# Residual additions of a decoder layer done by accumulating DMAs from GpSimd instead of loads and VectorE additions

## The chip, the core and the metric

The kernel runs on one core of a Trainium2 chip. The core has a matrix engine (TensorE, PE in the profile), three engines for elementwise work (VectorE DVE, ScalarE ACT, GpSimd POOL), and a queue engine, SyncE (SP), that here only starts transfers. Each engine runs its own list of instructions strictly in order and waits on semaphores for others. Transfers are carried by 16 DMA engines; what an engine's list holds is only the start of a transfer. Data lies in SBUF as 128 partitions by so many elements. The metric is the device time of one execution in microseconds.

## The reference

One decoder layer in float32: 1024 tokens, width 1024, one batch. A token mixer with three branches (pooling, a linear-attention recurrence, cross-attention into 256 memory tokens) is merged by gates and projected by `w_o`; then a gated feed-forward part with a short convolution follows. Both parts end in a norm and a residual addition; these two additions are what the change touches:

```python
merged = gates[:, :, 0] * y_pool + gates[:, :, 1] * y_rwkv + gates[:, :, 2] * y_mem
x = x + rms_norm(merged @ w_o[l], norm_mix_post[l])
h = rms_norm(x, norm_ffn_pre[l])
u = causal_dwconv(h @ w_ffn_up[l], conv_w[l], conv_b[l])
u_gate, u_val = jnp.split(u, 2, axis=-1)
f = (jax.nn.gelu(u_gate, approximate=True) * u_val) @ w_ffn_down[l]
x = x + rms_norm(f, norm_ffn_post[l])
```

## The kernel before

Activations are kept transposed, channels on the partitions: a tensor of 1024 channels and 512 tokens is eight blocks of 128 x 512. The tokens go in two halves, n = 0 and n = 1. Every product is made of three TensorE passes: weights and activations are split into a high part in a matmul type (`whi`, `h2h`, `mgh`) and the rest (`wlo`, `h2l`, `mgl`). A weight tile of 128 x 256 comes in by a load on SP (`wraw`, line 152), ScalarE casts it to `whi` (line 126), GpSimd subtracts to make `wlo` (line 129), and TensorE multiplies (lines 163 to 165). Two sets of such tiles alternate, three deep for `wraw` and four deep for `whi` and `wlo`.

Around the first residual the order in the program is: `merge(0)` and `wo_gemm(0)` make the eight blocks `o` of the first half; then `merge(1)` for the second half runs block by block (gate products on VectorE at lines 879 and 880, their split into `mgh` on ScalarE and `mgl` on VectorE, lines 119 and 120), and the generator `wo_residual(0)` is driven between its blocks. It takes the norm's factor `rs` (ones-matmul at line 1025, ScalarE at line 195), and for each of eight blocks k: scales `o[k]` (VectorE, line 1061), adds the block of the input x (line 1063) loaded into one of two buffers `xt` (SP, line 1060), stores the sum to DRAM as `d_x1` (SP, line 1064), and takes its square (ScalarE, lines 1016 and 1019) into a running sum `s2` (VectorE, line 1020). This is place A, 1337 to 1362 us.

`wo_residual(1)` does the same for the second half, beside the first tiles of the up projection (weights `in_w_fup`); there x comes as one load of 2 MB into `xts` (line 1054). This is place B, 1419 to 1450 us. `wo_norm` then scales `o` and splits it into `h2h` and `h2l`.

The tail, place C, 2110 to 2154 us: `down_pass` has left the first half's sums in `accs[0]`. While the last blocks of the second half run on TensorE (`half_down`), VectorE scales the eight blocks of `accs[0]` (line 1306), adds the stored `d_x1` (line 1307), which a load of 2 MB brought in long before (line 1292), and SP stores them to the output (line 1308).

The program text is not the order of the lists: the Tile layer schedules each engine's instructions by dependences, by priority in the text and by its own estimate of when each is ready. Buffers are rotated by tags, and a waiting instruction holds everything behind it on its engine.

Of the kernel before, what the change touches and what calls it, by code (L numbers as in the profile page):

```python
# [8 lines left out]
F32 = mybir.dt.float32  # L9
FR = mybir.dt.float32r  # L10
AF = mybir.ActivationFunctionType
ALU = mybir.AluOpType
# [4 lines left out]
P = 128  # L17
T = 1024
D = 1024
KC = D // P  # L20
# [22 lines left out]
def trunk_kernel(ctx: ExitStack, tc: tile.TileContext, xT, memT, pvec, w_in, w_kv, w_upd, w_upg,  # L43
                 w_pool, w_ppool, w_pmem, w_prwkv, w_o, w_fup, w_fdn, out):
    nc = tc.nc
    V, A, G, PE, SP = nc.vector, nc.scalar, nc.gpsimd, nc.tensor, nc.sync
# [9 lines left out]
    def dtile(shape, name):  # L56
        return dram.tile(shape, F32, name=name, tag=name)
# [7 lines left out]
    d_x1 = dtile([8, P, T], "d_x1")  # L65
# [6 lines left out]
    def col(name, i):  # L72
        o, w = PV[name]
        return pv[:, o + i:o + i + 1]
# [18 lines left out]
    for lo in (0, 64):  # L93
        s = slice(lo, lo + 64)
# [3 lines left out]
    for lo in (0, 64):  # L98
        s = slice(lo, lo + 64)
# [119 lines left out]
    for k in range(KC):  # L219
        tag = ("X01", "X11", "HV", "HV")[k // 2]  # L220
        if k in (0, 2, 4):
            xt = rw.tile([P, 4 if k == 4 else 2, T], F32, name=f"xr{k}", tag=tag)
# [560 lines left out]
    for hd in range(4):  # L783
        for t0, _ in HALVES:
            s = slice(t0, t0 + 512)
# [49 lines left out]
    for j in range(8):  # L835
        ws = load_w(w_pmem[j], 4)
        for n, (t0, _) in enumerate(HALVES):
            s = slice(t0, t0 + 512)
# [4 lines left out]
    for j in range(8):  # L843
# [4 lines left out]
        for n, (t0, _) in enumerate(HALVES):  # L848
            s = slice(t0, t0 + 512)
# [161 lines left out]
    ow = ow_ctx.enter_context(tc.tile_pool(name="ow", bufs=1))  # L1011
    h2h, h2l = [], []

    def sumsq(acc, src, first, eng):
        if first:
            A.activation(acc, src, AF.Square)
        else:
            sq = wp.tile([P, 512], F32, name="sq", tag="st", bufs=3)[:, :src.shape[-1]]
            A.activation(sq, src, AF.Square)
            eng.tensor_tensor(acc, acc, sq, op=ALU.add)  # L1020

    def norm(pool, acc, after=None):
        w = acc.shape[-1]
        ps = pss.tile([P, 512], F32, name="psn", tag="s")[:, :w]
        mm = PE.matmul(ps, ones, acc, start=True, stop=True)
        if after is not None:
            tc.add_manual_dep(mm.ins, after.name, nosync, reason="order")
        rs = pool.tile([P, 512], F32, name="rs", tag="rs", bufs=1)[:, :w]
        rstd(rs, ps, 0)
        return rs  # L1030
# [15 lines left out]
    def wo_residual(n, after=None):  # L1046

        s = slice(n * 512, n * 512 + 512)
        o = os_[n]
        rs = norm(ow, sss[n], after)  # L1050
        s2 = ow.tile([P, 512], F32, name="s2", tag="ss", bufs=2)
        if n:
            xts = hf.tile([P, KC, 512], F32, name="xts", tag="h2h1")
            SP.dma_start(xts, xT[:, s].rearrange("(k p) t -> p k t", p=P))
        for k in range(KC):
            if n:
                xt = xts[:, k]
            else:
                xt = ow.tile([P, 512], F32, name="xt", tag="xt", bufs=2)
                SP.dma_start(xt, xT[k * P:(k + 1) * P, s])  # L1060
            V.scalar_tensor_tensor(o[k], o[k], col("g_mix_post", k), rs, op0=ALU.mult,
                                   op1=ALU.mult)
            V.tensor_tensor(o[k], o[k], xt, op=ALU.add)
            SP.dma_start(d_x1[k][:, s], o[k])
            sumsq(s2, o[k], k == 0, V)
            if k % 2:
                yield s2
# [25 lines left out]
    merge(1, range(1, 3))  # L1093
    table(LN_EXP)
    res = wo_residual(0, pin)
    s2 = next(res)
    table(SIGMOID)
# [4 lines left out]
    hf = ctx.enter_context(tc.tile_pool(name="hf", bufs=1, side="right"))  # L1102
# [7 lines left out]

    pairs = [[first(0)]]
    res = wo_residual(1, last_mm[0])
    s2 = next(res)
    pairs[0].append(first(NF))
# [136 lines left out]
    def half_down(n, h, j, last):  # L1251

        qs = slice(256 * h, 256 * h + 256)
        ps = psg.tile([P, 2, 256], F32, name="psg", tag=f"g{j // 2 % 2}")
        for e in range(2):
            gemm(weights(j + e), hidden(n, qs), ps=ps[:, e])
        a_ = accs[n][:, j:j + 2, qs]
        V.tensor_tensor(a_, a_, ps, op=ALU.add)
        sq = wp.tile([P, 2, 256], F32, name="sq", tag="st", bufs=3)
        ss = ss3[1 - h].rearrange("p (e t) -> p e t", e=2)  # L1260
        if j == 0:
            A.activation(ss, a_, AF.Square)
        else:
            A.activation(sq, a_, AF.Square)
            if not last:
                V.tensor_tensor(ss, ss, sq, op=ALU.add)
        for e in range(2):
            A.activation(a_[:, e], a_[:, e], AF.Identity, scale=col("g_ffn_post", j + e))
        return ss, sq
# [20 lines left out]
    def load_x1(n):  # L1290
        t = hf.tile([P, KC, 512], F32, name="xt", tag=("h2h1", "h2l1")[n])
        SP.dma_start(t, d_x1[:, :, n * 512:n * 512 + 512].rearrange("k p t -> p k t"))
        return t

    down_pass(0)
    down_pass(4)
    xts = [load_x1(n) for n in range(2)]

    rs0 = None
    for j in range(0, 8, 2):  # L1300
        parts = half_down(1, 0, j, False)
        if j == 0:
            rs0 = norm(fa, ss3[0], last_mm[0])
        for k in range(j, j + 2):
            a_ = accs[0][:, k]
            V.scalar_tensor_tensor(a_, a_, col("g_ffn_post", k), rs0, op0=ALU.mult, op1=ALU.mult)
            V.tensor_tensor(a_, a_, xts[0][:, k], op=ALU.add)
            SP.dma_start(out[k * P:(k + 1) * P, 0:512], a_)
    for j in range(0, 8, 2):
        last = half_down(1, 1, j, j == 6)  # L1310
# [52 lines left out]
def build(arrays):  # L1363
    import numpy as np
    import concourse.bacc as bacc

    nc = bacc.Bacc("TRN2", target_bir_lowering=False, num_devices=1)
    aps = {n: nc.dram_tensor(f"in_{n}", a.shape, mybir.dt.from_np(a.dtype), kind="ExternalInput").ap()
           for n, a in arrays.items()}
    out = nc.dram_tensor("out_T", (D, T), F32, kind="ExternalOutput").ap()  # L1370
    with tile.TileContext(nc) as tc:
        trunk_kernel(tc, **aps, out=out)
    return nc
# [10 lines left out]
```

## Time and profile before

| what | us |
|---|---|
| median of 3 runs (2151.31 to 2157.1) | 2152.29 |
| the profiled execution | 2155.78 |
| its span | 2153.8 |
| TensorE busy | 2081.9 (97%) |
| VectorE busy | 1259.8 (58%) |
| ScalarE busy | 1048.6 (49%) |
| GpSimd busy | 825.0 (38%) |

The span is the time from the first to the last record of the execution; its own time is 2.0 us longer. The granted clock of TensorE was 0.989 of full speed on the mean. "Busy" counts the instructions that compute: the start of a transfer is not busy time on the engine that starts it. TensorE's matmuls are pipelined, so their lengths overlap; the distance of two starts tells the pace, 0.23 us for a matmul of 512 columns at full clock. A row of the timeline that ends in brackets tells how long the engine had been idle before, and which engine and line ended that.

### The profile page before, as it was taken

How to read it: one execution, taken by the hardware profiler on the slowest of the kernel's cores; microseconds unless marked ns; L12 is line 12 of the kernel's file. 1: busy time of each engine (PE TensorE's matmuls, PEld its weight loads, DVE VectorE, ACT ScalarE, POOL GpSimd, SP SyncE). 2: the span in 40 equal slices, each digit the busy share in tenths (PEclk: the TensorE clock that was granted, in tenths of full speed). 3: DMA queues.
4: the chain of work that ended last, by engine and by line, in shares of the span. 5: the costliest groups of instructions: out<-in, count | busy, mean ns of one | idle time of the engine just before them, and what ended most of it. 6: DMA issues, size and time to landing. Idle time of an engine off the chain costs nothing. (4 is left out here: it accounts for less than half of the span.)

```text
span 2153.8 us, 34571 instructions
## 1 busy us (share of the span) xinstructions
PE 2081.9 (97%) x12426; PEld 1594.7 (74%) x12426; DVE 1259.8 (58%) x2031; ACT 1048.6 (49%) x2241; POOL 825.0 (38%) x969
## 2 busy tenths in 40 slices
PE   7999999999999999999999999999999999989998
PEld 4777766776677676866777788777688777768887
DVE  6277437653656356734695434769677777732426
ACT  4584347623862376334565344446444444443423
POOL 6422112111212111201122355556688888843210
PEclk9999999999999999999999999999999999999999
DMA  4312111120212021214345343643322222275532
GB/s 145 131 39 80 61 63 58 63 72 30 89 55 87 21 84 59 89 42 165 127 138 173 123 131 119 189 135 113 105 74 86 76 74 88 75 236 157 162 103 79
DMA packets 170795, 215.04 MB, mean 100 GB/s; under 512 B 17408, under 2 KB 124544, under 8 KB 170624
## 3 DMA queue, kind: packets, MB, share of 16 engines
q1 hardware_dynamic: 170624, 212.84, 30.3%
q8 instruction: 98, 1.61, 0.3%
q14 instruction: 73, 0.60, 0.1%
HBM read 163.48 MB, written 49.28 MB: 99 GB/s over the span
## 5 line engine op out<-in xcount | busy, mean ns | idle before, releaser
L129 POOL TENSOR_TENSOR wlo<-wraw,whi 128x256 fp32r<-128x256 f32 x552 | 476.4, 870 | 1113.7 <-ACT whi L126 965.3
L126 ACT CAST whi<-wraw 128x256 fp32r<-128x256 f32 x560 | 219.6, 404 | 361.4 <-PE psg L164 159.1
L165 PE MATMUL psg<-hh,wlo 128*128 128x512 f32 x928 | 381.8, 411 | 7.3 <-POOL wlo L129 7.1
L163 PE MATMUL psg<-hh,whi 128*128 128x512 f32 x928 | 380.5, 410 | 0.0
L164 PE MATMUL psg<-hl,whi 128*128 128x512 f32 x928 | 378.3, 408 | 0.7 <-DVE hl L120 0.7
L165 PEld LDWEIGHTS psg<-hh,wlo 128*128 128x128 f32 x928 | 175.3, 189 | 54.7 <-POOL wlo L129 14.1
L163 PEld LDWEIGHTS psg<-hh,whi 128*128 128x128 f32 x928 | 175.3, 189 | 41.2 <-ACT tBN L195 0.8
L164 PEld LDWEIGHTS psg<-hl,whi 128*128 128x128 f32 x928 | 175.3, 189 | 40.9 <-DVE hl L120 1.3
L959 POOL TENSOR_TENSOR wt<-a,wt 128x256 fp32r<-128x256 f32 x136 | 133.8, 1012 | 28.7 <-ACT wt L958 28.7
L120 DVE TENSOR_TENSOR fl<-fraw,fh 128x512 fp32r<-128x512 f32 x82 | 61.3, 768 | 134.7 <-ACT fh L119 134.5
L163 PE MATMUL psd<-fh,whi 128*128 128x512 f32 x288 | 114.8, 399 | 9.0 <-DVE z L1004 9.0
L164 PE MATMUL psd<-fl,whi 128*128 128x512 f32 x288 | 114.7, 398 | 1.4 <-POOL fl L120 1.4
L165 PE MATMUL psd<-fh,wlo 128*128 128x512 f32 x288 | 114.5, 398 | 0.0
L959 POOL TENSOR_TENSOR wt<-sm,wt 128x256 fp32r<-128x256 f32 x102 | 106.7, 1065 | 14.5 <-ACT wt L958 14.2
L165 PE MATMUL psf<-h2h,wt 128*128 128x512 f32 x272 | 108.4, 398 | 1.3 <-POOL wt L959 1.2
L163 PE MATMUL psf<-h2h,wt 128*128 128x512 f32 x272 | 106.9, 393 | 1.2 <-ACT wt L958 1.2
L164 PE MATMUL psf<-h2l,wt 128*128 128x512 f32 x272 | 106.8, 393 | 0.0
L977 DVE SCALAR_TENSOR_TENSOR d<-z,pv,d 128x1023 f32<-128x1023 f32 x68 | 91.3, 1342 | 23.8 <-ACT d L975 11.4
L958 ACT CAST wt<-sm 128x256 fp32r<-128x256 f32 x102 | 37.9, 404 | 117.6 <-POOL sm L944 112.6
L165 PE MATMUL psf<-t,wt 128*128 128x512 f32 x204 | 81.2, 398 | 2.1 <-POOL wt L959 1.8
L164 PE MATMUL psf<-t,wt 128*128 128x512 f32 x204 | 80.3, 394 | 0.0
L163 PE MATMUL psf<-t,wt 128*128 128x512 f32 x204 | 80.2, 393 | 0.0
(403 smaller groups left out, 4596.0 us busy)
## 6 DMA issues: line engine op xcount, KB each, us to landing
wraw<-in_w_in SPq DMA_DIRECT2D x240, 128.0 KB, 2.3
fraw<-d_f SPq DMA_DIRECT2D x84, 256.0 KB, 3.1
a<-in_w_fup SPq DMA_DIRECT2D x128, 128.0 KB, 2.4
d_zg<-st SPq DMA_DIRECT2D x48, 256.0 KB, 2.7
wraw<-in_w_fdn SPq DMA_DIRECT2D x88, 128.0 KB, 2.4
wraw<-in_w_fup SPq DMA_DIRECT2D x80, 128.0 KB, 2.4
d_f<-d SPq DMA_DIRECT2D x17, 512.0 KB, 3.3
wraw<-in_w_prwkv SPq DMA_DIRECT2D x64, 128.0 KB, 2.3
```

Source lines behind the costliest of these rows:

```text
L120: return (lo_eng or V).tensor_tensor(lo, src, hi.bitcast(F32), op=ALU.subtract)
L126: A.copy(hi, src)
L129: (V if lo_on_dve[0] else G).tensor_tensor(lo, src, hi.bitcast(F32), op=ALU.subtract)
L163: first = PE.matmul(ps, wh, xh, start=start, stop=False)
L164: PE.matmul(ps, wh, xl, start=False, stop=False)
L165: last_mm[0] = PE.matmul(ps, wl, xh, start=False, stop=stop).ins
L958: A.copy(w[0][:, us], src[u])
L959: G.tensor_tensor(w[1][:, us], src[u], w[0][:, us].bitcast(F32), op=ALU.subtract)
L977: V.scalar_tensor_tensor(d[:, n:], z[:, :T - n], col(cw, j), d[:, n:], op0=ALU.mult, op1=ALU.add)
```

## The change

In `wo_residual` and in the tail, the loads of x (or of `d_x1`) into SBUF and the VectorE additions go. Instead GpSimd starts, for each block, a transfer of 128 x 512 from DRAM that adds what it reads to the block in SBUF (`accum_op=ALU.add`). That is 24 loads and additions in all, in 10 load instructions, replaced by 24 transfers. The stores and squares that followed the additions now follow the transfers' landing. In `xts` of the tail only the second half's load is left.

```diff
@@ -1049,18 +1049,10 @@
         o = os_[n]
         rs = norm(ow, sss[n], after)
         s2 = ow.tile([P, 512], F32, name="s2", tag="ss", bufs=2)
-        if n:
-            xts = hf.tile([P, KC, 512], F32, name="xts", tag="h2h1")
-            SP.dma_start(xts, xT[:, s].rearrange("(k p) t -> p k t", p=P))
         for k in range(KC):
-            if n:
-                xt = xts[:, k]
-            else:
-                xt = ow.tile([P, 512], F32, name="xt", tag="xt", bufs=2)
-                SP.dma_start(xt, xT[k * P:(k + 1) * P, s])
             V.scalar_tensor_tensor(o[k], o[k], col("g_mix_post", k), rs, op0=ALU.mult,
                                    op1=ALU.mult)
-            V.tensor_tensor(o[k], o[k], xt, op=ALU.add)
+            G.dma_start(o[k], xT[k * P:(k + 1) * P, s], accum_op=ALU.add)
             SP.dma_start(d_x1[k][:, s], o[k])
             sumsq(s2, o[k], k == 0, V)
             if k % 2:
@@ -1294,7 +1286,7 @@
 
     down_pass(0)
     down_pass(4)
-    xts = [load_x1(n) for n in range(2)]
+    xts = [None, load_x1(1)]
 
     rs0 = None
     for j in range(0, 8, 2):
@@ -1304,7 +1296,7 @@
         for k in range(j, j + 2):
             a_ = accs[0][:, k]
             V.scalar_tensor_tensor(a_, a_, col("g_ffn_post", k), rs0, op0=ALU.mult, op1=ALU.mult)
-            V.tensor_tensor(a_, a_, xts[0][:, k], op=ALU.add)
+            G.dma_start(a_, d_x1[k][:, 0:512], accum_op=ALU.add)
             SP.dma_start(out[k * P:(k + 1) * P, 0:512], a_)
```

The change also moves instructions in the lists. GpSimd's list at A and B, the two lists compared (a minus stands for before, a plus for the change; line 1055 of the changed kernel is the new transfer, `wlo` are the weight splits):

```order
-L129 TENSOR_TENSOR wlo<-wraw,whi 128x256 x206
...
+L129 TENSOR_TENSOR wlo<-wraw,whi 128x256 x108
+L1055 DMA o<-in_xT 128x512 x6
+L129 TENSOR_TENSOR wlo<-wraw,whi 128x256 x3
+L1055 DMA o<-in_xT 128x512
+L129 TENSOR_TENSOR wlo<-wraw,whi 128x256
+L1055 DMA o<-in_xT 128x512
+L129 TENSOR_TENSOR wlo<-wraw,whi 128x256 x53
+L1055 DMA o<-in_xT 128x512 x6
+L129 TENSOR_TENSOR wlo<-wraw,whi 128x256 x2
+L1055 DMA o<-in_xT 128x512
+L129 TENSOR_TENSOR wlo<-wraw,whi 128x256
+L1055 DMA o<-in_xT 128x512
```

What was one run of 206 splits is now cut by two groups of eight transfers, of which six each stand without a split between them.

At A, the same list of the changed kernel by buffer numbers (`wlo_13275` to `wlo_13293` are the four tiles of one weight block in the order in which TensorE reads them, `wlo_13344` to `wlo_13356` belong to the next block):

```order
L129 TENSOR_TENSOR wlo_13275<-wraw_13273,whi_13274 128x256
L129 TENSOR_TENSOR wlo_13281<-wraw_13279,whi_13280 128x256
L129 TENSOR_TENSOR wlo_13287<-wraw_13285,whi_13286 128x256
L1055 DMA o_12522<-in_xT 128x512
L129 TENSOR_TENSOR wlo_13344<-wraw_13342,whi_13343 128x256
L1055 DMA o_12522<-in_xT 128x512
L129 TENSOR_TENSOR wlo_13350<-wraw_13348,whi_13349 128x256
L129 TENSOR_TENSOR wlo_13356<-wraw_13354,whi_13355 128x256
L129 TENSOR_TENSOR wlo_13293<-wraw_13291,whi_13292 128x256
```

The block's last tile, `wlo_13293`, now stands behind all eight transfers and behind three tiles of the next block.

At B, SP's list before (`d_x1` are the stores of the residual, `wraw` the weight loads of the up projection, `a21` a load for later):

```order
L1064 DMA d_x1_81<-o_13480 128x512 x2
L152 DMA wraw_14274<-in_w_fup 128x256
L935 DMA a21_15221<-in_w_fup 128x512
L152 DMA wraw_14280<-in_w_fup 128x256
L1064 DMA d_x1_81<-o_13481 128x512
L152 DMA wraw_14231<-in_w_fup 128x256
L1064 DMA d_x1_81<-o_13481 128x512
L152 DMA wraw_14364<-in_w_fup 128x256
```

And the same place of the changed kernel (line 1056 is the store; the weight `wraw_14213` here is `wraw_14231` above, since the buffer numbers differ by 18 there):

```order
L1056 DMA d_x1_81<-o_13464 128x512
L935 DMA a21_15203<-in_w_fup 128x512
L1056 DMA d_x1_81<-o_13464 128x512
L1056 DMA d_x1_81<-o_13465 128x512 x2
L1056 DMA d_x1_81<-o_13466 128x512 x2
L1056 DMA d_x1_81<-o_13467 128x512 x2
L152 DMA wraw_14213<-in_w_fup 128x256
L152 DMA wraw_14250<-in_w_fup 128x256
```

The stores now stand together, and the load of `wraw_14213` and the loads after it stand behind all eight; before, loads stood between the stores.

## Rows read from the trace of the kernel before

**Rows 1.** The page: engines' busy time, data queue, weight cast, up-projection loads.

```profile
PE 2081.9 (97%) x12426; PEld 1594.7 (74%) x12426; DVE 1259.8 (58%) x2031; ACT 1048.6 (49%) x2241; POOL 825.0 (38%) x969
...
q1 hardware_dynamic: 170624, 212.84, 30.3%
...
L126 ACT CAST whi<-wraw 128x256 fp32r<-128x256 f32 x560 | 219.6, 404 | 361.4 <-PE psg L164 159.1
...
wraw<-in_w_fup SPq DMA_DIRECT2D x80, 128.0 KB, 2.4
```

**Rows 2.** Stretches: length, busy us (and instructions) of each engine, granted clock, DMA.

```profile
1337.00:1362.00 25.00, 25.00 (x109) 20.07 (x108) 23.93 (x32) 16.41 (x34) 14.90 (x14) 1.00 0.67 214
1362.00:1380.00 18.00, 15.72 (x59) 11.77 (x58) 7.98 (x10) 6.11 (x16) 11.37 (x14) 0.91 0.87 276
1419.00:1450.00 31.00, 30.43 (x128) 23.66 (x127) 25.28 (x36) 15.08 (x33) 17.73 (x20) 1.00 0.48 158
2110.00:2141.00 31.00, 30.89 (x225) 28.91 (x223) 22.94 (x37) 15.10 (x30) 0.00 (x0) 1.00 0.19 73
```

**Rows 3.** Timeline of TensorE, 1367 to 1375: start, length, operation, [idle before, releaser].

```profile
1367.55 0.39 PE L165 MATMUL psg<-mgh,wlo 128*128 128x512 f32 x1
1369.49 0.49 PE L163 MATMUL psg<-mgh,whi 128*128 128x512 f32 x1 [1.56 <-ACT mgh L119]
1370.71 0.70 PE L164 MATMUL psg<-mgl,whi 128*128 128x512 f32 x1 [0.72 <-DVE mgl L120]
...
1374.46 0.40 PE L164 MATMUL psg<-mgl,whi 128*128 128x512 f32 x1
```

**Rows 4.** Timeline of VectorE just before that wait.

```profile
1367.06 1.21 DVE L880 TENSOR_TENSOR g<-g,pm 128x512 f32<-128x512 f32 x1
```

**Rows 5.** Instructions on tile o: ns min/median/max, first and last start; its stores' landing.

```profile
L1061 DVE SCALAR_TENSOR_TENSOR o<-o,pv,rs x16: 739/744/1326, 1337.1 to 1442.0; 128x512 f32<-128x512 f32 x16
L1063 DVE TENSOR_TENSOR o<-o,xt x8: 678/684/1229, 1338.5 to 1360.2; 128x512 f32<-128x512 f32 x8
L1063 DVE TENSOR_TENSOR o<-o,xts x8: 675/938/1225, 1425.9 to 1445.0; 128x512 f32<-128x512 f32 x8
L1064 SPq DMA_DIRECT2D d_x<-o x16: 326/327/1048, 1339.2 to 1446.8; - x16
...
DMA to landing us min/median/max: 2.0/2.8/4.0
```

**Rows 6.** Instructions on tile xt, same columns; its loads' landing.

```profile
L1307 DVE TENSOR_TENSOR acc<-acc,xt x8: 684/684/685, 2123.6 to 2135.4; 128x512 f32<-128x512 f32 x8
...
DMA to landing us min/median/max: 3.4/3.9/10.2
```

**Rows 7.** GpSimd's timeline before A, in A and in B; then its groups by shape.

```profile
1334.55 0.73 POOL L129 TENSOR_TENSOR wlo<-wraw,whi 128x256 fp32r<-128x256 f32 x1 [0.66 <-ACT whi L126]
1340.90 11.51 POOL L129 TENSOR_TENSOR wlo<-wraw,whi 128x256 fp32r<-128x256 f32 x10 [5.62 <-ACT whi L126]
...
1424.10 2.42 POOL L129 TENSOR_TENSOR wlo<-wraw,whi 128x256 fp32r<-128x256 f32 x2 [1.48 <-ACT whi L126]
...
L120 POOL TENSOR_TENSOR fl<-fraw,fh 128x512 fp32r<-128x512 f32 x2 | 3.0, 1515 | 0.0
```

**Rows 8.** Timeline of SP's queue in A.

```profile
1342.29 4.51 SPq L152 DMA_DIRECT2D wraw<-in_w_prwkv  x4
```

**Rows 9.** Timeline of TensorE at four moments: in A, in B twice, at the end.

```profile
1350.78 0.39 PE L165 MATMUL psg<-yh,wlo 128*128 128x512 f32 x1
...
1440.50 0.39 PE L163 MATMUL psg<-h2h,whi 128*128 128x512 f32 x1
...
1448.23 1.13 PE L1025 MATMUL psn<-s,ones 128*128 128x512 f32 x2 [0.57 <-DVE s L1020]
...
2140.94 0.28 PE L165 MATMUL psg<-fh,wr 128*128 128x256 f32 x1
```

**Rows 10.** The chain that ended last, near its end: start, length, engine, tile, line.

```profile
2142.07 0.61 DVE acc L1258
```

## The prediction

> **What bounds the kernel now.** I read the page's busy times first, then the tables by stretch at the three changed places, then the rows of the waiting engine in each. TensorE is busy 2081.9 us of the 2153.8 us span [rows 1], so an edit counts only where it makes TensorE wait or ends a wait. The three places, by the table of stretches [rows 2]:
>
> - Place A (first residual, 1337 to 1362): TensorE 25.00 of 25 us, so nothing is lost inside. VectorE is busy 23.93 of them and falls behind. The price is paid afterwards: in 1362 to 1380 TensorE has 15.72 of 18 us and the granted clock averages 0.91.
> - Place B (second residual, 1419 to 1450): TensorE 30.43 of 31; VectorE 25.28, GpSimd 17.73.
> - Place C (tail, 2110 to 2141): TensorE 30.89 of 31, VectorE 22.94, GpSimd nothing.
>
> The wait behind A stands in [rows 3]: matmuls start 0.23 us apart, then one starts 1.94 us after its forerunner, the next 1.22 later, and the nine starts after that take 3.75 us where 2.10 would do (the engine sat idle, and the clock came back at its lower level of 1.2 GHz for these). From 1367.55 to 1374.46 there are eleven steps: 6.91 us against 2.56, a loss of **4.4 us**. The named releasers are the gate products of the last block (mgh, mgl), and [rows 4] shows VectorE at their input, line 880, until 1368.27, though TensorE had long gone on to the next product: VectorE's backlog from A is what is late.
>
> **The change part by part.** Each place gives up eight VectorE additions and its loads, and gains eight GpSimd accumulating DMAs. Two unknowns carry the sum: *g*, GpSimd's time for one such DMA, and *L*, the time from there to its landing. The trace holds no GpSimd DMA; the data queue listed is the hardware one [rows 1].
>
> Bounds for g: below, an issue on SP at 0.33 us [rows 5]; a crowded SP spends 4.51 us over four, 1.13 each [rows 8]; above, GpSimd's own pass over a tile of this size, 1.5 us [rows 7]. Below nothing is excluded: an issue takes the engine's time. I take **g = 1.2**, next to the crowded issues, for it writes a description of the tile rather than touch all of it. For L: this tile's stores land in 2.0 to 4.0 us, median 2.8 [rows 5], the x blocks in 3.4, 3.9 and 10.2 [rows 6]. An accumulation has to read both sides, so I take **L = 3.5**, between the two medians; the bounds are 2.0 and 10.2. The Trainium skill ("DMA: Bandwidth & Descriptors", the section on the anatomy of a GpSimd DMA) fits 2.0 us plus bytes over 436 GB/s for such a transfer: an estimate of 2.6 us for 256 KB. No run here shows it; with 2.6 for L place B would come out 0.9 us cheaper, and A unchanged.
>
> *Place A, what goes.* Eight additions, 0.68 to 1.23 us each [rows 5], some 5.8 us, out of a stretch in which VectorE has 1 us free. Its backlog of about 5 us goes, and with it the 4.4 us wait: gain **−4.4**. What is late next there is GpSimd's row.
>
> *Place A, what comes.* GpSimd issues in order. Six DMAs stand in a row ahead of three weight splits, then one, a split, one, and three splits more up to the tile wlo_13293. The first DMA can begin when the first scaled block is ready, 1337.1 + 0.74 = 1337.9 [rows 5]. A split takes 0.73 us with VectorE quiet and 1.15 (ten in 11.51) beside it [rows 7]; I take 1.0, as VectorE has eight operations fewer. So the eighth DMA and seven splits end at 1337.9 + 8g + 7.0. TensorE first reads that tile at 1350.8 [rows 9]. Wait: 8g + 7.0 − 12.9 = 8g − 5.9, which is **3.7 us** at g = 1.2, nothing below 0.74, 6.1 at 1.5. A wait of this length seems to bring the low clock behind it, as in [rows 3]: there the nine slow steps cost 3.75 − 2.10 = **1.7**. Sum of A: −4.4 + 3.7 + 1.7 = **+1.0**. SP's queue waits there too (stores to d_x1 stand behind landings, two weight loads among them), but the loads concerned are read later than this GpSimd tile, so it hides beneath. The eight sums of squares on VectorE now wait for landings and stand ahead of gate products; by the last landing, about 1355, VectorE has the freed 5 us to absorb that.
>
> *Place B, what goes.* The additions, 0.68 to 1.23 each [rows 5], and the 2 MB load. On TensorE's path only the wait of the norm's matmul, 0.57 [rows 9]: **−0.6**. The later waits of 1450 to 1480 hang on a block's own end and stay.
>
> *Place B, what comes.* SP now holds eight d_x1 stores in a row, each waiting for its accumulation's landing, and behind them every further weight load of the up projection; before, the loads stood between the stores. The path: the first DMA starts when GpSimd has made one split, 1424.10 + half of 2.42 = 1425.3, say 1425.4 [rows 7]. Eight DMAs with three splits among them (0.8 each) end at 1427.8 + 8g, and the last lands L later. Then the store's issue and the load's, 0.4 each [rows 5], the load's landing, 2.4, and the cast, 0.4 [rows 1]: 3.6 in all. TensorE reads that weight at 1440.5 [rows 9]. Wait: 1427.8 + 8g + L + 3.6 − 1440.5 = 8g + L − 9.1, which is **4.0** at the chosen values, nothing at g = 0.6 with L = 3.5, 6.9 at 1.5 and 4.0. With the slow clock behind it, 1.7: B = −0.6 + 4.0 + 1.7 = **+5.1**.
>
> *Place C.* Eight additions of 0.68 us go [rows 6], but TensorE sets this stretch, 30.89 of 31 [rows 2]. At its end the last addition of a block from PSUM stands on the chain at 2142.07 [rows 10], while its matmuls ended at 2140.94 + 0.28 = 2141.22 [rows 9]: 0.85 us in VectorE's queue, of which I leave 0.15 for the handover: **−0.7**. The DMAs stand in an idle GpSimd queue, and the stores behind them have some 15 us before the last stores: cover, unless eight of them take over 15 us, after which each further microsecond would count.
>
> *Sum:* +1.0 + 5.1 − 0.7 = **+5.4 us**. Against the profiled execution, 2155.8 (its span of 2153.8 and 2.0 around it), that is 2161.2; the median, 2152.3, lies 3.5 below that execution, so I state **2157.7**. That is 0.25%, and 0.3% (6.5 us) is about what a measurement of this kernel can tell from no change.
>
> **Rivals.**
> 1. *Cheap issue.* With g up to 0.6 and L about 3 no queue makes TensorE wait and VectorE's relief is all that is left: −4.4 − 0.6 − 0.7 = −5.7, so **2146.6**. For it: SP's 0.33 us. Against it: those are hardware issues, and four in a row already cost SP 1.13 each.
> 2. *Queues blocked behind the accumulations* (slower). The place is SP in B: loads behind eight stores that wait for landings. From 8g + L = 9.1 each microsecond of it is one of TensorE. At g = 1.5, L = 4.0: A 6.1 + 1.7 − 4.4 = 3.4, B 6.9 + 1.1 = 8.0, C −0.7: +10.7, **2163.0**. At L = 10.2, as the slowest x block took, B is 13.1 + 1.1 = 14.2, and A's SP path (8g + L + four splits − 15.9, 10.3) gives 7.6: +21.1, **2173.4**. For it: all landings share the engines with a weight stream. Against it: 10.2 was one of eight.
> 3. *GpSimd held up by VectorE.* A split takes 1.15 us beside VectorE's two-input operations and 0.73 without them [rows 7], so GpSimd work does stretch there. If the DMA's issue stretches as much, by 1.58 to 1.9 us: A 15.2 − 5.9 + 1.7 − 4.4 = 6.6, B 15.2 + 3.5 − 9.1 + 1.1 = 10.7, C −0.7: +16.6, **2168.9**. The Trainium skill ("SBUF — State Buffer", the section on who interferes with whom) says that a VectorE operation in a two-port mode locks GpSimd out, so it can't write descriptors, while one with two inputs in SBUF contends only with GpSimd's reads. By that rule the scalings at A and B wouldn't hold the DMAs; the splits, which read, are held, and [rows 7] agrees with that part.
> 4. *No effect.* Both waits stay just under their cover while the backlog behind A stays too (the sums of squares wait for landings and take the additions' place): A 0, B 0, C −0.7: **2151.6**.
>
> **How the numbers follow.** Forecast (g of 0.9 to 1.4): 0.46. It runs from −1.8 (g = 0.9, L = 3.0: A 1.3 + 0.5 − 4.4 = −2.6, B 1.1 + 1.0 − 0.6 = 1.5, C −0.7, with part of the slow clock for short waits) to +8.8 (g = 1.4, L = 3.7: A 2.6, B 6.9, C −0.7); a quarter of it lies over +6.5. Cheap issue 0.16, of which a third may pass −6.5. Blocked queues 0.20, GpSimd held up 0.08, no effect 0.10. Slower: 0.12 + 0.20 + 0.08 = 0.40; faster: 0.05, and 0.03 for a relief that reaches further waits: 0.08; the rest 0.52. The range runs from the cheap issue to the middle of the blocked queues and the hold-up: 2146.5 to 2172.
>
> **What would show it.** A GpSimd DMA near 1.2 us and landings near 3.5 show the terms. Right: the wait at 1369 gone, a wait of 2 to 5 us on a GpSimd split near 1350, another near 1440 on a cast that waits for an up-projection load, SP's stores in B standing in a row. Wrong: g under 0.7 (then rival 1); landings far above 4 us or GpSimd's splits starved (rivals 2, 3); or the wait at 1369 still there, which would mean that the gate products were late for another reason than the additions.

## The result and the profile of the changed kernel

The changed kernel takes 2160.55 us (median of 11, 2155.4 to 2167.47), the kernel before 2152.29 in the same comparison: a ratio of 1.0038, 95% interval 1.0028 to 1.0049, some 8.2 us slower. The forecast was 2157.7 with a range of 2146.5 to 2172, and "within 0.3%" as the likeliest outcome (0.52, against 0.40 for slower); the time lies in the range, 2.9 us above the forecast, and on the slower side of that bound with most of its interval.

The page, parts 1 and 3, answers to [rows 1]. There is a second data queue now:

```profile
PE 2081.6 (96%) x12426; PEld 1596.3 (74%) x12426; DVE 1245.3 (58%) x2007; ACT 1049.5 (49%) x2241; POOL 838.8 (39%) x993
...
q1 hardware_dynamic: 167392, 206.55, 29.5%
q0 software_dynamic: 3456, 6.29, 1.7%
```

TensorE's work is the same (2081.6 us), in a span of 2158.4 instead of 2153.8. GpSimd's 24 starts of transfers are counted among its instructions here (993, 969 before), unlike those of SP. The 24 accumulations moved 6.29 MB and took 1.7% of the 16 engines' span; everything else moved 206.55 MB in 29.5%. Per megabyte that is 0.27 against 0.143: an accumulated byte costs 1.9 times a plain one.

The three places by stretches, same columns as [rows 2] (the last two are the share of the 16 DMA engines and GB/s; a share can pass 1.00 a little, since it is the sum of the times that packets took):

```profile
1335.00:1354.00 19.00, 12.48 (x55) 9.71 (x53) 15.23 (x17) 9.06 (x20) 13.02 (x15) 0.93 1.00 227
1362.00:1380.00 18.00, 18.00 (x78) 14.44 (x77) 6.24 (x8) 6.53 (x17) 11.76 (x16) 1.00 0.37 110
1419.00:1450.00 31.00, 24.71 (x100) 18.93 (x99) 16.78 (x24) 12.73 (x26) 17.03 (x20) 0.90 0.78 193
1450.00:1480.00 30.00, 27.89 (x106) 21.66 (x106) 22.68 (x34) 17.74 (x38) 19.25 (x21) 0.90 0.35 103
2110.00:2146.00 36.00, 35.89 (x246) 32.91 (x245) 21.42 (x35) 16.63 (x33) 6.94 (x8) 1.00 0.47 107
2130.00:2146.00 16.00, 16.00 (x133) 15.89 (x132) 13.45 (x23) 9.03 (x20) 5.47 (x7) 1.00 1.06 239
```

The first of them in the kernel before:

```profile
1335.00:1354.00 19.00, 19.00 (x83) 15.29 (x82) 17.27 (x22) 11.79 (x24) 11.79 (x11) 1.00 0.62 196
```

In place A TensorE now works 12.48 of 19 us, where it lost nothing before, and the DMA share is 1.00 where it was 0.62. In place B it works 24.71 of 31 instead of 30.43. The stretch 1362 to 1380 is full (18.00; before 15.72), and so is the tail. VectorE did get its relief: 16.78 us in B instead of 25.28.

The waits, on TensorE's timeline:

```profile
1353.93 0.80 PE L163 MATMUL psg<-yh,whi 128*128 128x512 f32 x1 [6.52 <-ACT whi L126]
...
1447.87 0.79 PE L163 MATMUL psg<-h2h,whi 128*128 128x512 f32 x1 [6.29 <-ACT whi L126]
...
1476.63 0.50 PE L165 MATMUL psg<-h2h,wlo 128*128 128x512 f32 x1 [2.11 <-POOL wlo L129]
```

Two waits of 6.5 and 6.3 us on a cast of weights, each with a stretch of steps 0.43 us apart behind it (granted clock 0.50, so 1.2 GHz), are new. Both wait for a load that SP issued late. SP's timeline in A and in B:

```profile
1339.61 5.82 SPq L1056 DMA_DIRECT2D d_x<-o  x4
1345.52 0.89 SPq L152 DMA_DIRECT2D wraw<-in_w_prwkv  x1
...
1431.65 12.24 SPq L1056 DMA_DIRECT2D d_x<-o  x7
1443.97 16.25 SPq L152 DMA_DIRECT2D wraw<-in_w_fup  x19
```

And ScalarE's, with the cast that TensorE waits for:

```profile
1353.47 0.40 ACT L126 CAST whi<-wraw 128x256 fp32r<-128x256 f32 x1 [3.68 <-DMA wraw<-in_w_prwkv]
...
1447.41 0.75 ACT L126 CAST whi<-wraw 128x256 fp32r<-128x256 f32 x2 [3.15 <-DMA wraw<-in_w_fup]
```

In A four stores, each waiting for its accumulation, spread over 5.8 us; the load behind them starts at 1345.52, and its cast at 1353.47. That load took 7.9 us, where loads of this size land in 2.4 [rows 1]: the DMA engines are full, and the store started just ahead of it took as long (8.2 us). It is the longest in the view of the weight tiles from 1340 to 1358:

```profile
DMA to landing us min/median/max: 2.9/3.1/7.9
```

In B seven stores spread over 12.2 us, the load starts at 1443.97, lands 3.4 us later, and TensorE goes on at 1447.87.

The accumulations themselves, in the view of tile o for both residuals (GpSimd's rows, then those of SP, the stores):

```profile
L1055 POOL DMA_DIRECT2D o<-in_xT x16: 845/1386/2503, 1335.1 to 1434.9; - x16
DMA to landing us min/median/max: 4.5/7.8/11.5
...
L1056 SPq DMA_DIRECT2D d_x<-o x16: 319/323/637, 1339.6 to 1443.6; - x16
DMA to landing us min/median/max: 3.2/7.4/10.7
```

and in the view of tile acc for the tail (the second row is the output store, which waits for the accumulation):

```profile
L1299 POOL DMA_DIRECT2D acc<-d_x x8: 844/964/1087, 2128.5 to 2136.4; - x8
L1300 SPq DMA_DIRECT2D out_T<-acc x8: 332/332/338, 2132.2 to 2146.0; - x8
```

An accumulation lands 7.8 us after its issue (median; 4.5 to 11.5), and the stores, which took 2.8 before [rows 5], now take 7.4. The tail shows the pace: GpSimd issued its eight between 2128.5 and 2136.4, one each microsecond, but the stores that wait for them start between 2132.2 and 2146.0, seven steps in 13.8 us. One accumulation of 256 KB follows another at **2.0 us**; in A and B it is 1.9 and 2.1 on the mean, with single steps of 1.3 to 3.2.

The DMA engines have no room for more: from the first packet of eight accumulations to the last, their share is 1.04 to 1.07 in each of the three places by the packet records, 0.71 to 0.81 of it the accumulations. One of them is eight packets of 178 ns for each engine, 1.4 us; most of the rest of the 2.0 is plain transfers, in the tail nearly all output stores.

TensorE's matmuls stand in the same order in both kernels up to the tail, so the same matmul can be compared in both traces. How much later it starts in the changed kernel:

| matmul of the kernel before, us | later by, us | what lies between |
|---|---|---|
| 1236 to 1350.1 | −3.05 | the two executions differ by that before the change begins |
| 1352.4 | +5.5 | the new wait in A and its slow clock: +8.6 |
| 1418.6 | +0.9 | the wait of [rows 3] is gone: −4.7 (−4.4 at the wait itself) |
| 1443.5 | +10.1 | the new wait in B and its slow clock: +9.2 |
| 1469.4 | +3.4 | the norm's wait at 1448 (−0.7) and waits at 1462 and 1464 are gone, with their slow clock: −6.7 in all |
| 1473.8 | +6.9 | a new wait at 1476.6 (changed kernel) with slow clock: +3.5 |
| 2131 | +5.2 | small differences: −1.7 |
| 2143.4 | +4.4 | the tail: −0.7 |

A costs 3.9, B 6.0, and 2.4 come back later: 7.5 us between the two profiled executions once the offset at the start is taken out, against 8.2 between the medians.

### The profile page after: what moved, and what is told of

Its sections match the earlier page's. It is cut to its first block, busy times and chain, and to the rows that moved or that the text cites. A ratio compares the mean times of both kernels' runs of the same rounds, so it can differ in the third digit from the quotient of the medians.

```text
span 2158.4 us, 34598 instructions
## 1 busy us (share of the span) xinstructions
PE 2081.6 (96%) x12426; PEld 1596.3 (74%) x12426; DVE 1245.3 (58%) x2007; ACT 1049.5 (49%) x2241; POOL 838.8 (39%) x993
## 3 DMA queue, kind: packets, MB, share of 16 engines
q1 hardware_dynamic: 167392, 206.55, 29.5%
q0 software_dynamic: 3456, 6.29, 1.7%
## 5 line engine op out<-in xcount | busy, mean ns | idle before, releaser
L959 POOL TENSOR_TENSOR wt<-sm,wt 128x256 fp32r<-128x256 f32 x102 | 106.7, 1065 | 14.4 <-ACT wt L958 14.2
L977 DVE SCALAR_TENSOR_TENSOR d<-z,pv,d 128x1023 f32<-128x1023 f32 x68 | 91.2, 1341 | 23.9 <-ACT d L975 11.5
```

Source lines behind the costliest of these rows:

```text
L959: G.tensor_tensor(w[1][:, us], src[u], w[0][:, us].bitcast(F32), op=ALU.subtract)
L977: V.scalar_tensor_tensor(d[:, n:], z[:, :T - n], col(cw, j), d[:, n:], op0=ALU.mult, op1=ALU.add)
```

## The experiments

All ratios are against the kernel before, timed beside each on the same chip, with 95% intervals. The edits are shown in excerpts.

**The three places apart.** e3 keeps the change at A alone, e4 at B alone, e9 in the tail alone:

```diff
 # e3 (e4 with the condition reversed, and the other half's load and addition kept)
+            if n:
+                V.tensor_tensor(o[k], o[k], xts[:, k], op=ALU.add)
+            else:
+                G.dma_start(o[k], xT[k * P:(k + 1) * P, s], accum_op=ALU.add)
 # e9: only the tail's part of the change
-            V.tensor_tensor(a_, a_, xts[0][:, k], op=ALU.add)
+            G.dma_start(a_, d_x1[k][:, 0:512], accum_op=ALU.add)
```

> The accumulation in the first residual only; second residual and tail as before. Theory: the wait of 6.5 us and its slow clock, less the 4.4 us wait at 1369 that goes: +4 us, 2156 (ratio 1.002). Rival: the places act on each other and one alone costs the whole 8 us, or nothing.

> The accumulation in the second residual only; first residual and tail as before. Theory: the wait of 6.3 us and a slow clock of 2.8, less some 3 us of waits at 1462 to 1466 that go or move: +5 us, 2157 (ratio 1.0025). Rival: nothing (within 2 us), the cost of the change being that of the first place.

> The accumulation in the tail only; both residuals before it as in the kernel before. Theory: TensorE sets this stretch, the eight accumulations land within 16 us on an idle GpSimd queue, and only the 0.7 to 1 us of VectorE's queue at the end is won: median 2150 to 2152.5, ratio 0.9985 to 1.0005. Rival: the output stores of the first half, which wait for landings, hold those of the second half on SP and lengthen the end: 2153.5 or more, ratio above 1.001.

Measured: e3 1.0021 (1.0008 to 1.0035), 4.5 us; e4 1.0026 (1.0015 to 1.0036), 5.6 us; e9 1.0000 (0.9990 to 1.0010). A and B cost what the comparison of the traces says, they add up within their intervals (0.47% against 0.38%), and the tail is worth nothing that can be measured. The waits stand in each alone: 5.35 us at 1353.20 in e3, 6.41 at 1444.02 in e4.

**Is it the accumulation or GpSimd's queue?** e1 makes the transfers plain loads, in the tail too; every engine's order stays that of the changed kernel.

```diff
-            G.dma_start(o[k], xT[k * P:(k + 1) * P, s], accum_op=ALU.add)
+            G.dma_start(o[k], xT[k * P:(k + 1) * P, s])
```

> The 24 GpSimd transfers become plain loads: they overwrite the blocks with x instead of adding to them (so both residual sums are left out), and the order of every engine is that of the changed kernel. Theory: what costs is the accumulation itself, since its packets of 2 KB take 178 ns where plain loads of that size take 84, and the accumulations land one after another, 2.0 us apart, so that the eighth is there 18 us after the first issue; SP's stores wait for that and the weight loads behind them are late. Then the eighth plain transfer lands within about 10 us of the first issue, the waits of 6.5 us at 1354 and 6.3 us at 1448 are gone (under 1 us each), and the median is 8 to 14 us under the changed kernel's 2160.5: 2146 to 2152. Rival: the price is that of any transfer which GpSimd issues (its descriptors, its one queue). Then the spacing stays near 2 us, both waits stay at 5 to 7 us and the median is 2158 to 2163.

Measured: 2152.17, 0.9996 (0.9983 to 1.0010), some 9 us under the changed kernel's ratio. The page's row of the GpSimd queue in e1:

```profile
q0 software_dynamic: 1920, 6.29, 0.9%
```

its transfers in the view of tile o (GpSimd's rows):

```profile
L1055 POOL DMA_DIRECT2D o<-in_xT x16: 536/538/732, 1336.2 to 1429.0; - x16
DMA to landing us min/median/max: 3.1/5.1/7.3
```

and TensorE's waits in A and B:

```profile
1349.35 0.50 PE L163 MATMUL psg<-yh,whi 128*128 128x512 f32 x1 [0.91 <-ACT whi L126]
...
1440.84 0.79 PE L163 MATMUL psg<-h2h,whi 128*128 128x512 f32 x1 [2.92 <-ACT whi L126]
```

The plain transfers take 0.9% of the engines' span for the same bytes, as loads do, half of the accumulations' 1.7%; GpSimd is busy 0.54 us with one instead of 0.85 and more; the wait in A falls to 0.9, that in B to 2.9. So the accumulation decides; with it goes the packet size, since the plain transfers have half as many packets (1920 on the page, 3456 before), of 4 KB. Not all of the theory held: the wait in B is not under 1, and the last transfer of B still lands 14.4 us after the first issue (1421.3 to 1435.7), where under 10 was expected and 19.0 are taken by the accumulations. Most of that is what stands between the issues and in the queue; the accumulation adds some 4.5 us. And with no addition at all, neither on VectorE nor in a transfer, e1 is not faster than the kernel before.

**Which queue holds TensorE?** e2 and e5 take the stores' wait for landings off SP in two ways, e6 takes the squares' wait off ScalarE, e7 does both (e5 and e6 together).

```diff
 # e2: the store of another tile
-            SP.dma_start(d_x1[k][:, s], o[k])
+            SP.dma_start(d_x1[k][:, s], rs)
 # e5: the store moved ahead of the norm, into wo_gemm
             V.tensor_copy(os_[n][j], ps)
+            SP.dma_start(d_x1[j][:, s], os_[n][j])
...
-            SP.dma_start(d_x1[k][:, s], o[k])
 # e6: the square of another tile
-            sumsq(s2, o[k], k == 0, V)
+            sumsq(s2, rs, k == 0, V)
```

> The 16 stores to d_x1 store the norm's factor instead of the sum (so what the tail adds is wrong in value, the same bytes are moved), so that no store waits for a landing; the accumulations stay. Theory: the waits of TensorE come from SP, where weight loads stand behind stores that wait for landings. Then the wait at 1354 falls from 6.5 to at most 2 us and that at 1448 from 6.3 to at most 2 us, and the median is 2146 to 2153. Rival: the casts on ScalarE stand behind squares that wait for the same landings, and that alone holds TensorE. Then the waits stay at 4 us or more and the median is 2156 or more.

> The d_x1 stores are made earlier, each right behind the block's copy out of PSUM, from the block before its norm (so the tail adds other values; the same bytes are stored, spread over the earlier products). SP then waits for no landing; the squares on ScalarE still do. Theory of two queues: the accumulations land one after another, 2.0 us apart, and both SP (loads behind stores) and ScalarE (casts behind squares) stand behind them; with SP freed, ScalarE still holds TensorE: waits of 3 to 6 us in each place, median 2155 to 2160. Rival: SP alone was the holder and the stores made at one go in the run before were what delayed the accumulations there; then the waits are under 2 us and the median is 2145 to 2151.

> The squares are taken of the norm's factor instead of the blocks (so the second norm gets another factor), so ScalarE waits for no landing; the stores on SP still do. Theory of two queues: SP's stores still hold the weight loads: waits of 3 to 6.5 us in each place, median 2154 to 2160. Rival: ScalarE alone was the holder; then the waits are under 2 us and the median is 2145 to 2151.

> Both edits of the two runs before together: neither SP nor ScalarE waits for an accumulation; these go on as in the changed kernel and the norms' scalings wait for them (the tail and the second norm get other values). Theory of two queues: the waits in both places fall under 1.5 us, the 4.4 us wait at 1369 stays away, and the median is 2143 to 2149, under the kernel before. Rival: the accumulations hurt by loading the DMA engines, or by GpSimd's issue time ahead of its splits; then waits of 3 us or more remain and the median is 2153 or more.

Measured: e2 1.0032 (1.0013 to 1.0050), e5 1.0025 (1.0009 to 1.0040), e6 1.0013 (0.9995 to 1.0031), e7 1.0017 (1.0002 to 1.0033). The four can't be told from each other by their times, and e6 not from the kernel before; what follows rests on the waits. TensorE's rows with a wait in A and in B, for e2, e5, e6 and e7 in this order:

```profile
1358.12 0.79 PE L163 MATMUL psg<-yh,whi 128*128 128x512 f32 x1 [5.41 <-ACT whi L126]
...
1446.78 0.80 PE L163 MATMUL psg<-h2h,whi 128*128 128x512 f32 x1 [4.66 <-ACT whi L126]
```

```profile
1348.11 0.50 PE L163 MATMUL psg<-yh,whi 128*128 128x512 f32 x1 [0.91 <-ACT whi L126]
1350.13 0.51 PE L165 MATMUL psg<-yh,wlo 128*128 128x512 f32 x1 [1.29 <-POOL wlo L129]
...
1443.22 0.50 PE L163 MATMUL psg<-h2h,whi 128*128 128x512 f32 x1 [1.35 <-ACT whi L126]
```

```profile
1352.37 0.50 PE L163 MATMUL psg<-yh,whi 128*128 128x512 f32 x1 [3.00 <-ACT whi L126]
...
1448.43 0.50 PE L163 MATMUL psg<-h2h,whi 128*128 128x512 f32 x1 [1.91 <-ACT whi L126]
```

```profile
1352.17 0.50 PE L163 MATMUL psg<-yh,whi 128*128 128x512 f32 x1 [0.40 <-ACT whi L126]
...
1371.48 0.50 PE L163 MATMUL psg<-mgh,whi 128*128 128x512 f32 x1 [1.23 <-ACT mgh L119]
1372.70 0.50 PE L164 MATMUL psg<-mgl,whi 128*128 128x512 f32 x1 [0.72 <-DVE mgl L120]
...
1422.19 1.28 PE L1025 MATMUL psn<-ss,ones 128*128 128x512 f32 x2 [3.48 <-DVE ss L1020]
...
1448.72 0.50 PE L165 MATMUL psg<-h2h,wlo 128*128 128x512 f32 x1 [0.81 <-POOL wlo L129]
...
1469.96 0.50 PE L163 MATMUL psg<-h2h,whi 128*128 128x512 f32 x1 [3.18 <-ACT whi L126]
```

The waits, changed kernel 6.5 and 6.3: with SP freed 0.9 + 1.3 and 1.4 (e5), with ScalarE freed 3.0 and 1.9 (e6), with both 0.4 and 0.8 (e7). The accumulations go on in all of them, in e7 even to a later end than in the changed kernel (4.0 us in A, 3.4 in B, by the packet records and reckoned from TensorE's matmuls). So neither their load on the DMA engines nor GpSimd's issue time makes TensorE wait by itself; it takes the lists that stand behind their landings. By the waits, e2 came out as its rival has it, e5 too (under 2 us, though its time did not), e6 as its theory has it in A and not in B.

In A two things add up. TensorE waits for one load of 128 KB there. Reckoned from TensorE's matmuls, SP starts it 4.4 us later in the changed kernel than in e7, and it lands 7.9 us after its start, in e7 6.2. The 4.4 of SP's list and the 1.7 of the landing are the difference of the two waits (6.5 and 0.4). With the stores moved, e5 and e7 take 2 MB of stores out of each place, so they relieve the DMA engines too, not SP alone. In B the load lands 3.4 us after its start, so there it is chiefly SP's list.

How much ScalarE's squares hold is less clear, since the edits also move the accumulations. In e2 the eight stores start in one burst; in A the same load then starts as early as in e7, but takes 9.1 us to land, so that of the 5.4 us only some 1.9 are ScalarE's. In B the cast that TensorE waits for stands right behind a square that waited for its accumulation, and by the order of loads and casts its own load had landed at least 6 us before: there the squares alone hold TensorE for 4.7 us. In e5 the 0.9 in A is again the load, the 1.4 in B the squares. Neither list alone is the cause; ScalarE's is a few microseconds behind SP's.

e7 fails its expectation in the sum: the median stays 0.17% above the kernel before, not under it. By the same matmuls as in the table above it starts 1.3 us late ahead of A, 0.4 behind it, and then loses 4.8 us from 1418 to 1421, on a sum of squares (the wait of 3.5 at 1422, also in e5, 2.9 at 1417.8). Both have the moved stores there: the weight load right behind such a store lands 3.9 to 4.1 us after its start in e7, where the loads of this stretch took 2.2 to 3.0 before, and ScalarE's casts and squares come late behind them. B costs e7 1.0 us. Without that side effect and the wait that follows at 1470 (3.2, the one at 1462 in the kernel before, 1.3) it would stand about where the kernel before stands; that is reckoned from the trace and not run.

Why nothing is won behind A stands in its two rows at 1371.5 and 1372.7: 1.2 + 0.7 us, the wait of [rows 3] (1.6 + 0.7), although VectorE has no residual addition left and TensorE comes only 1.0 us later there than ahead of A. The expectation that this wait stays away failed.

**Fewer, larger accumulations.** e8 accumulates two blocks with one transfer of 512 KB; their two stores and squares follow it.

```diff
-            G.dma_start(o[k], xT[k * P:(k + 1) * P, s], accum_op=ALU.add)
+            if k % 2:
+                G.dma_start(pair[k // 2], xT[(k - 1) * P:(k + 1) * P, s]
+                            .rearrange("(k p) t -> p k t", p=P), accum_op=ALU.add)
```

> In both residuals one accumulation for two blocks (512 KB, 4 instead of 8; packets stay 2 KB); tail as in the changed kernel. Theory: of the 2.0 us from one accumulation to the next 8 packets of 178 ns per engine are 1.4 and the rest is paid once per transfer; four of 2.8 + 0.5 us land in 13.5 us instead of 16, the waits fall by some 2.5 us each, median 2154 to 2157. Rival: the whole 2.0 us goes by bytes; then the last landing and the waits stay and the median is 2159 to 2163.

Measured: 2161.39, 1.0037 (1.0020 to 1.0055); the waits are 7.28 and 4.98.

```profile
1355.66 0.80 PE L163 MATMUL psg<-yh,whi 128*128 128x512 f32 x1 [7.28 <-ACT whi L126]
...
1448.33 0.80 PE L163 MATMUL psg<-h2h,whi 128*128 128x512 f32 x1 [4.98 <-ACT whi L126]
```

Its landings in the view of tile o (GpSimd's rows):

```profile
DMA to landing us min/median/max: 5.7/8.3/10.8
```

By the packet records the bytes of A take 13.5 us from the first to the last, as the theory had it, instead of 15.8; but the first can begin only when two blocks are scaled, two microseconds later (1338.9 instead of 1336.8), and a block is there only when its pair is. Neither wait falls by the 2.5 us of the theory, and the time is the rival's. A wait that grows in A and shrinks in B suggests that the landing of single blocks counts, not the last one alone; no run parts the two.

**A smaller dose.** e10 accumulates blocks 0 to 3 of each residual, e11 blocks 0 and 1; the others are loaded and added as before, the tail as before. e12 is e10 with the casts to `mgh` of the last two gate blocks moved from ScalarE to VectorE.

```diff
 # e10 (e11: 2 for 4)
+            if k >= 4:
+                V.tensor_tensor(o[k], o[k], xt, op=ALU.add)
+            else:
+                G.dma_start(o[k], xT[k * P:(k + 1) * P, s], accum_op=ALU.add)
 # e12, in merge
+            if n == 1 and j >= 6:
+                V.tensor_copy(mgh[j][:, s], gt)
+                V.tensor_tensor(ml_, gt, mgh[j][:, s].bitcast(F32), op=ALU.subtract)
```

> In both residuals blocks 0 to 3 are accumulated by GpSimd, blocks 4 to 7 are loaded and added on VectorE as before; tail as before. Theory: four accumulations, 2.0 us apart, are all there some 10 us after the first issue, when SP and ScalarE need no more of them than before, so that the waits of 6.5 and 6.3 us shrink to at most 1.5 us, while VectorE is relieved of four additions in each place and the 4.4 us wait at 1369 falls by 2 to 4.4: median 2147 to 2151 (ratio 0.9965 to 0.9995). Rival: any accumulation in these places costs its landing: a wait of 3 us or more stays in each place, 2154 to 2158.

> As the run before, with blocks 0 and 1 alone accumulated. Theory: no wait from landings, two additions less in each place, the 4.4 us wait at 1369 falls by 1 to 2: median 2149 to 2152 (ratio 0.9975 to 1.0). Rival: the first landing (4.5 us after issue, where an addition took 0.7) alone is what costs: then this is as slow as with four, 2154 or more.

> As e10 (blocks 0 to 3 accumulated in both residuals), and the casts to mgh of the last two gate blocks are done by VectorE instead of ScalarE. In e10 and e7 the wait behind the first residual (1.8 and 0.7 us, with a slow clock) came back although VectorE had four or eight additions less. Theory: that wait is ScalarE's, whose casts to mgh stand behind casts of weights that wait for loads; moved to VectorE, the casts pass that queue and the wait falls from 1.8 + 0.7 to under 0.7 in all; the median is 0.9975 to 0.9995 of the kernel before. Rival: the wait follows from VectorE's chain of gate products itself, which now gets two operations more: it stays at 1.5 us or more and the ratio is 0.9995 to 1.002.

Measured: e10 1.0005 (0.9992 to 1.0019), e11 1.0006 (0.9994 to 1.0017), e12 0.9998 (0.9984 to 1.0012): none can be told from the kernel before, and none has the gain of its theory. TensorE's waits behind A in e10:

```profile
1364.19 0.50 PE L163 MATMUL psg<-mgh,whi 128*128 128x512 f32 x1 [1.82 <-ACT mgh L119]
1365.41 0.78 PE L164 MATMUL psg<-mgl,whi 128*128 128x512 f32 x1 [0.72 <-DVE mgl L120]
```

ScalarE's timeline there:

```profile
1362.91 0.71 ACT L126 CAST whi<-wraw 128x256 fp32r<-128x256 f32 x2 [1.56 <-POOL wlo L129]
1363.53 0.61 ACT L119 CAST mgh<-g 128x512 fp32r<-128x512 f32 x1
```

The same in e11, VectorE's last gate product and ScalarE's timeline:

```profile
1359.04 1.19 DVE L880 TENSOR_TENSOR g<-g,pm 128x512 f32<-128x512 f32 x1
...
1361.26 0.71 ACT L126 CAST whi<-wraw 128x256 fp32r<-128x256 f32 x2 [3.46 <-DMA wraw<-in_w_o]
1361.88 0.61 ACT L119 CAST mgh<-g 128x512 fp32r<-128x512 f32 x1
```

TensorE's only wait at that place in e12:

```profile
1364.93 0.50 PE L164 MATMUL psg<-mgl,whi 128*128 128x512 f32 x1 [0.44 <-DVE mgl L885]
```

In e10 the waits of 6 us are gone (no wait over 0.4 us in A or B), so four accumulations are covered. But the wait behind A is still there, 1.8 + 0.7, although VectorE has four additions less and stands idle for 3.6 us shortly before, until ScalarE's cast of the block ahead. In e11, with two additions less, it has even grown, to 3.4 + 0.4. Both theories, which had it fall, failed there. ScalarE's rows tell what it is: the cast to `mgh` stands behind two weight casts, which waited for GpSimd to free a buffer (e10) or for a load (e11); in e11 VectorE's product had ended 1.6 us before that cast began, in e10 only 0.1. With the last two of these casts on VectorE (e12) the wait is 0.44 in all, and TensorE's matmuls come 3.6 us earlier behind it. So this wait is that of ScalarE's list, as the theory of e12 said; its second half, a median below that of the kernel before, is not shown (0.9998): by 1480 small waits, the first of 1.1 us at 1412, have taken 2.6 of the 3.6 us back. Whether the moved casts would do it without the four accumulations was not tried.

## Why the prediction came out as it did

The direction and the range were right, the account only in part, and some of the nearness is luck: in A the gain came for another reason than the one given, and in B two errors nearly cancelled. Of the prediction's own signs, the wait at 1369 is gone, a wait near 1440 on a cast behind an up-projection load is there, and SP's stores stand in a row in B; the wait near 1350 is there, but not on a GpSimd split. One of its signs of being wrong came too, landings far above 4 us, which it gave to rivals 2 and 3; what rival 2 describes, loads held behind the accumulations, is what the runs show in both places.

- **The landing, L.** This is the term that was mis-sized, by its form. L counts from the end of GpSimd's part: 3.5 us taken, and the first accumulation of A and of B took 3.4 and 3.7. But the prediction let every accumulation land L after its own issue, paced by GpSimd's g, and they land at 2.0 us apart: 6.5 in the median of the sixteen, 9.0 at the most. The prediction had 8g + L + 2.4 = 15.5 us from the first issue to the last landing in B; it was 19.0 (1424.6 to 1443.6, the last store). The rival "queues blocked" with the middle of its landings (2163.0) was about as near as the forecast.
- **The issue, g.** 1.2 taken; 0.85 at the least and 1.39 as the median measured, and six in a row start 0.66 us apart. It didn't matter, since landings at 2.0 us apart are the slower pace. The rival that VectorE holds the issues up (2.5 us at the longest) stays without weight for the same reason. "DMA: Bandwidth & Descriptors" of the Trainium skill (the section on the anatomy of a GpSimd DMA) gave 2.6 us for one transfer as an estimate. Of e1's plain transfers the fastest landed 3.1 us after its start, 2.5 after GpSimd's part, so it fits that one; their median is 5.1 from the start, and no row agrees with it for accumulations in a row.
- **Place A, what comes.** The tile was the right one, the engine wrong. The prediction named GpSimd's split of wraw_13291's tile and said that SP's wait hides beneath it, the loads concerned being read later. It is the cast of the same tile that waits, for a load issued behind four stores and 7.9 us under way; 6.5 us instead of 3.7, and 8.6 with the slow clock instead of 5.4. Full DMA engines, which stretched that load, are in no term of the sum.
- **Place A, what goes.** The −4.4 came in the trace too, for a reason that was not the stated one: luck. The prediction read the wait behind A as VectorE's backlog. e7 has no addition left and the wait is back at 1.2 + 0.7; e10 has half and it is 1.8 + 0.7; e12 moves two casts off ScalarE and it is 0.4. In the changed kernel it vanished because TensorE itself came 8.6 us later, so that the loads and casts had caught up: a later wait covered by an earlier one. It is gone in e3 as well, and in e4, which leaves A alone, it is there (1.8 + 0.6). ScalarE's timeline of the kernel before, which the prediction did not read, has the second chain:

```profile
1368.21 0.71 ACT L126 CAST whi<-wraw 128x256 fp32r<-128x256 f32 x2 [1.79 <-DMA wraw<-in_w_o]
1368.83 0.61 ACT L119 CAST mgh<-g 128x512 fp32r<-128x512 f32 x1
```

VectorE's line 880 ended at 1368.27 [rows 4]; the cast to `mgh` could not start before 1368.8 anyway, behind two weight casts that waited for a load. Two chains ended within 0.6 us, and the prediction read one.
- **Place B.** The mechanism was right, loads behind stores that wait for landings, with its price at 9.2 instead of 5.7 through L. The −0.6 of the norm's wait came out (−0.7). The statement that the later waits of 1450 to 1480 stay was wrong: they lost 6.0 us to the same covering, and 3.5 came back as a new one. e3, without B's change, has the waits at 1462 and 1464 (1.5 and 1.9), e4 has neither.
- **Place C.** −0.7 forecast, −0.7 in the trace, too little for e9's interval to show. The eight accumulations took longer than the cover of some 15 us, 17.4 from the first issue to the last landing; the second half's first stores stood behind that on SP until 2146.4, but the last store, at 2154.9, did not.
- **The sum.** +1.0 + 5.1 − 0.7 = +5.4 forecast, +3.9 + 6.0 − 1.7 − 0.7 = +7.5 by the traces. A was 2.9 us too cheap; B only 0.9, since a price 3.5 us too small met later waits that it covered, which the forecast did not have; −1.7 is small differences behind B.

What stays open: whether the accumulations would follow one another faster on emptier engines. The engines were full in all three places; in e5, without the stores beside them, the first six of a place land 1.6 us apart, not 1.9, which fits that account. Several queues were not tried.

## What to carry to other kernels

A transfer that replaces a cheap operation is to be priced by when its result is there, and by the pace of a row of them, not by what its issue costs; then look at each in-order list that has an instruction waiting for it, and at what stands behind, and at whether the DMA engines have room for both. Before a wait is credited to a change, check that the engine named is alone in ending it: two chains that end within half a microsecond may mean that removing one gains nothing. A wait that vanishes behind a new, longer one has been covered, not removed, and only a run without the new one tells.

## What the runs showed of the hardware

An accumulating transfer of 256 KB from DRAM into SBUF by GpSimd follows its forerunner at 2.0 us, with stores beside it and the DMA engines full; its packets of 2 KB take 178 ns (median, packet records) where plain loads of the same size take 84, and it holds GpSimd for 0.85 us at the least, against 0.54 for a plain transfer. Eight of them beside stores and a stream of weights filled the DMA engines (share 1.00) and stretched a load of 128 KB from 2.4 to 7.9 us, without the stores to 6.2 (e7). And one of VectorE's scalings took far longer than any before, once in place A of either kernel, while GpSimd issued and split, with accumulations and with plain transfers (3.24 us in the changed kernel, 3.03 in e1, 0.74 in the median):

```profile
L1053 DVE SCALAR_TENSOR_TENSOR o<-o,pv,rs x16: 732/746/3243, 1334.1 to 1428.4; 128x512 f32<-128x512 f32 x16
```

```profile
L1053 DVE SCALAR_TENSOR_TENSOR o<-o,pv,rs x16: 740/744/3027, 1335.1 to 1425.1; 128x512 f32<-128x512 f32 x16
```

Nothing here shows what held it.
